# A long convolution's gates turned by VectorE through device memory, and its second inverse transform and norm done by rows

## The chip, the core and the metric

The kernel runs on one core of one Trainium2 chip. The core has five engines that run side by side and wait for each other by semaphores: TensorE (PE in the profile, with its weight loads as PEld) multiplies matrices, VectorE (DVE) and ScalarE (ACT) work elementwise, GpSimd (POOL) here mostly issues DMAs, and SyncE (SP) issues the other DMAs. Each engine takes its instructions in one fixed order; an instruction that waits holds everything behind it on the same engine. The metric is the device time of the whole program in microseconds (us). Times of the kernel before are the median of three runs.

## What is computed

One block of an encoder over 256 positions and 2048 features, in f32: a mix of four groups of 512 features each, then cross attention, then a gated feed-forward network, then a norm. The change touches the third group, a Hyena mixer:

```python
def hyena_mixer(u, conv_w, filt, skip):
    u = short_conv(u, conv_w).astype(jnp.float32)
    v, x1, x2 = jnp.split(u, 3, axis=-1)
    z = x1 * long_conv(v, filt[0], skip[0])
    return x2 * long_conv(z, filt[1], skip[1])
...
y_c = rms_norm(hyena_mixer(u_h, hy_conv_w[l], filt, hy_skip[l]), grp_norm_g[l, 1])
...
x = x + mix @ w_out[l]
```

`long_conv` is a convolution over all positions, done by a transform, a product and an inverse transform. `rms_norm` divides each position by the root mean square of its 512 features and multiplies by a gain for each feature.

## The kernel before

**Weights.** All large products go through one stream of weights. `Stream._half` (L73 to L106) loads slabs of 1 MB (`raw`, issued by SP at L81, three buffers) and splits each f32 weight in two halves of fewer bits: ScalarE rounds to `wh` (L102) and VectorE subtracts to get `wl` (L103). TensorE then multiplies three times (high by high, high by low, low by high) and sums in PSUM. One half slab is a tile of 128x1024; three buffers of `wh` and `wl` and a fourth that every fourth half uses let the splits run up to three halves ahead of TensorE. `gemm` (L296, L297) gives results with features on the partitions and positions along the row; `gemm_rows` (`part_rows`, L345 to L347) gives positions on the partitions and features along the row.

**Order of the rest.** The small work of the mixers is written as generators that hand over control with `yield`. `Background.poll` is called between the weight products and runs a step of a generator when enough TensorE time has passed since its last one and when VectorE is not thought to be behind (`owed`, which grows with each VectorE instruction announced by `dve` and falls with the TensorE time announced by `pe`). `drain` runs a generator to its end at once. The program's builder then orders each engine's instructions and sets the semaphores, so that small work lands between the weight products on TensorE and between the splits on ScalarE and VectorE.

**Hyena before.** `gemm("w_in", ...)` computes 12 tiles of 128 features by 256 positions: v (tiles 0 to 3), x1 (4 to 7), x2 (8 to 11). Each goes to `Hyena.feed` (L1057), which applies the short convolution (`conv3`, L599). For tiles 0 to 7 it then turns the tile with two TensorE transposes (L1067), one for even and one for odd times, so that time is on the partitions: v is split into two halves for the transforms, x1 is copied by ScalarE (L1076) to the tile `x1`. x2 stays with features on the partitions. The generator `convs` (L1238) makes the first transform (`spectrum`, `dft`, `triple` at L1106), the first inverse transform (12 products of 128x512, L1247 to L1261), the product with `x1`, the second transform, and then the second inverse transform: 16 products in full f32 whose results have 128 columns (L1280), with features on the partitions again, times x2, into `res[0]`. `group_norm` (L606) sums the squares over partitions with products by ones (L244), takes the inverse root with some twelve tiny VectorE instructions (`rstd_cols`), spreads it over the partitions with two products of 256 columns (L280), scales by it and by the gain, and splits the result into `act[16:20]` (L206 on ScalarE, L198 on VectorE).

**After Hyena.** Three `gemm_rows` follow the tile products: the values and the queries and keys of the GLA group, and the input of the FNet group. The queries and keys are turned by VectorE within blocks of 32x32 (`store_turned`, L380), stored to device memory by POOL (L382) and fetched back in the order wanted (`Gla.fetch`, L1330, 16 loads by POOL). This way of turning by a VectorE transpose, a store and a load with short runs is used for many other tiles (L382 and L387). Then all generators are drained, the buffers of Hyena are given up, and `Gla.open` takes their place with new tiles: it loads `gkw` (L1315) and `masks` (L1316) on SP and clears two tiles by POOL (L1318 to L1320). `gkw` is the right side of the products at L1337 that open the GLA group. `Fnet.open` loads its tables on SP (L1488). Last, `out_proj` multiplies `act[16:20]` (Hyena) first, then the GLA and FNet groups, then the last group.

Of the kernel before, what the change touches and what calls it, by code (L numbers as in the profile page):

```python
# [13 lines left out]
F32 = mybir.dt.float32  # L14
# [3 lines left out]
AF = mybir.ActivationFunctionType  # L18
ALU = mybir.AluOpType
# [3 lines left out]
P = 128  # L23
R = 256
# [18 lines left out]
LAG, OWED, SOON, FAR = 1.3, 0.9, 0.01, 18.0  # L43
V_NG = 0
V_GRP = 64
V_GLA = 76
V_GKB = 77
V_HCW = 81
V_SCW = 117
# [120 lines left out]
class Block:  # L170
# [219 lines left out]
    def run(self):  # L390
        nc, cp = self.nc, self.cp
        st = self.st
        self.act = [cp.tile([P, 512], F32R, name=f"act{i}") for i in range(24)]
        self.res = [cp.tile([P, 4, R], F32, name=f"res{i}") for i in range(4)]
        self.resk = lambda i: self.res[i // 4][:, i % 4, :]
        self.vec = cp.tile([P, NV], F32, name="vec")
        self.onesr = cp.tile([P, P], F32R, name="ones")
        self.ones = self.onesr.bitcast(F32)
        self.ident = cp.tile([P, P], F32, name="ident")

        self.sq = [cp.tile([P, 8], F32, name=f"sq{i}") for i in range(2)]
        self.mg = cp.tile([P, 16], F32, name="mg")
        self.eps = cp.tile([P, 8], F32, name="eps")[:, 0:1]
        self.gap(cp, 416)

        self.kd = self.outside("keys", KT)
        self.xf = [self.outside(n, KT) for n in ("features1", "features2")]
        self.qf = self.outside("queries", KT)
        self.sf, self.gf, self.gq = (self.outside(n, 4) for n in ("products", "gates", "gla"))
        self.ff = self.outside("hidden", FT)  # L410
        self.vd = nc.dram_tensor("values", (P, 8 * 512), F32, kind="Internal").ap()
        def load(src, k, n):
            nc.sync.dma_start(self.res[k // 4][:, k % 4:k % 4 + n, :].rearrange("p k r -> p (k r)"),
                              self.t[src][:, k * R:(k + n) * R])

        self.load_x = lambda k, n: load("xT", k, n)

        nc.vector.memset(self.ones, 1.0)

        p = self.bank()  # L420
        for _ in range(10):
            nc.tensor.matmul(p[:, 0:P], self.ones, self.ones, start=True, stop=True)
        nc.vector.memset(self.eps, EPS)
# [13 lines left out]
    def mixers(self):  # L437
        tc, nc, act = self.tc, self.nc, self.act
# [85 lines left out]
        with tc.tile_pool(name="mid", bufs=1) as mid:  # L524
# [41 lines left out]
            with tc.tile_pool(name="glp", bufs=1) as glp:  # L566
                gl.open(glp)
                fn.open(glp)
                g_fn = self.bg.add(fn.mix(act[0:4], gl))
                g_gla = self.bg.add(gl.mix(act[4:8]))  # L570
                halves = [(r, j) for r in range(2) for j in range(0, 512, R)]
                ps = self.gemm_rows("w_in", [US + 512], h)[0]
                c = [self.tmp() for _ in halves]
                for t, (r, j) in zip(c, halves):
                    nc.scalar.copy(t, ps[r][:, j:j + R])
                ps = self.gemm_rows("w_in", [US + 1024], h)[0]
                for t, (r, j) in zip(c, halves):
# [12 lines left out]
                def ev_s(i, p):  # L590
                    u0.append(i)
                    self.merge(p, self.res[1][:, i, :])

                self.gemm("w_in", [US + i * P for i in range(4)], h, ev_s)
                gl.done = True
                return self.out_proj(lambda n: self.bg.drain((g_fn, g_gla, g_sc)[n]))

    def conv3(self, u, c, y=None):
        y = self.tmp() if y is None else y  # L599
# [426 lines left out]
class Hyena:  # L1026
# [5 lines left out]
    def __init__(self, b, pool, k2):  # L1032
        self.b, self.k2, self.ready, self.pending = b, k2, False, None
        tile_ = lambda n, s, dt=F32: pool.tile(s, dt, name=n)
        self.tab = tile_("tab", [P, 512])
        self.tabh, self.tabl = (tile_(n, [P, 512], F32R) for n in ("tabh", "tabl"))

        self.backh, self.backl = (tile_(n, [P, 2 * P], F32R) for n in ("backh", "backl"))
        self.sp = [[[tile_(f"sp{o}{c}{k}", [P, 512]) for k in range(2)] for c in range(2)] for o in range(2)]
        self.x1 = tile_("x1", [P, 2, 512])  # L1040
        self.x2 = [tile_(f"x2{i}", [P, R]) for i in range(4)]

    def piece(self):
        return self.k2.tile([P, 512], F32, name="k2", tag="k2")
# [15 lines left out]
    def feed(self, i, u):  # L1060

        b, nc = self.b, self.b.nc
        if self.pending is not None:
            j, y = self.pending
            p = b.bank()
            for t in range(2):
                nc.tensor.transpose(p[:, t * P:(t + 1) * P], y[:, t, :], b.ident)  # L1067
            pv = p[:, 0:R].rearrange("p (t c) -> p t c", t=2)
            s = slice((j % 4) * P, (j % 4 + 1) * P)
            if j == 0:  # L1070
                self.z = [self.pair() for _ in range(2)]
            if j < 4:
                for par in range(2):
                    b.split2(*(d[:, s] for d in self.z[par]), pv[:, par, :])
            else:
                nc.scalar.copy(self.x1[:, :, s], pv)  # L1076
            self.pending = None
        if i < 8:
            self.pending = i, b.conv3(u, V_HCW + 3 * i).rearrange("p (i two) -> p two i", two=2)
# [165 lines left out]
    def convs(self):  # L1245
        b, nc = self.b, self.b.nc
        while not self.ready:  # L1247
            yield
        yield from self.spectrum(0)
        while self.fed < 9:  # L1250
            yield
        ps = []
        for par in range(2):
            y = [self.halves(self.y[cs][par]) for cs in range(2)]
            yield
            ps.append(b.bank())
            for cs in range(2):
                o = (2 * cs + 1) * P if par else cs * P
                th, tl = (self.tabh, self.tabl) if par else (self.backh, self.backl)
                self.triple(ps[par], th[:, o:o + P], tl[:, o:o + P], *y[cs], cs == 0, cs == 1)  # L1260
            b.bg.pe(1.4)  # L1261
# [10 lines left out]
        out = b.res[0]  # L1272
        nat = lambda x: x.rearrange("p (i two) -> p two i", two=2)
        sq = []
        for j in range(4):
            p = b.bank()
            s = slice(j * P, (j + 1) * P)
            for par in range(2):
                for cs in range(2):
                    nc.tensor.matmul(p[:, par * P:(par + 1) * P], self.y[cs][par][:, s], self.table(cs, par),  # L1280
                                     start=cs == 0, stop=cs == 1)
            b.tt(nat(out[:, j, :]), p[:, 0:R].rearrange("p (two i) -> p two i", two=2), nat(self.x2[j]), ALU.mult)
            if j % 2:
                yield
        yield from b.group_norm(out, 1, b.act[16:20])


class Gla:
# [358 lines left out]
```

## Time and profile before

| | us |
|---|---|
| median of three runs | 1471.92 (1471.43 to 1472.27) |
| the profiled execution, its own time | 1471.97 |
| its span, from the first to the last instruction of the core | 1470.2 |
| TensorE busy in that span | 1460.1 |
| VectorE busy | 929.6 |
| ScalarE busy | 746.3 |
| GpSimd busy | 179.3 |

The profile page gives busy times, a strip of the span in 40 slices, the chain of waits that ended last, and the costliest groups. The trace behind it can be asked for windows (busy time of each engine in a stretch), for a timeline of one engine, for the instructions of one source line, for waits and for DMAs. In a timeline a line shows the start, the time of the merged instructions, the engine, the source line, the operation, `out<-in` by tile names, sizes, the count and, in brackets, the idle time before and what ended it. Matmuls overlap in their pipeline, so the distance from one start to the next, not the duration shown, is what a matmul costs.

### The profile page before, as it was taken

The page shows a single profiled execution, that of the slowest core. Times are in us where ns is not written, and L with a number is a line of the kernel's source. Part 1 is how long each engine was busy: PE and PEld are TensorE (multiplying, and loading weights), DVE is VectorE, ACT ScalarE, POOL GpSimd, SP SyncE. Part 2 cuts the span into 40 slices and gives each one's busy share as a digit, 9 for nine tenths or more (in the row PEclk, how much of TensorE's full clock was granted, in tenths as well). Part 3 has the DMA queues.
Part 4 walks back from the last instruction along what each step waited for, and adds up shares of the span by engine and source line. Part 5 has one row for each costly group of instructions (what it writes and reads, how often), then busy time and mean ns, then how long its engine had stood idle before and what let it go on. Part 6 is the DMA issues. An engine that isn't in the chain of part 4 may idle for free.

```text
span 1470.2 us, 18237 instructions
## 1 busy us (share of the span) xinstructions
PE 1460.1 (99%) x6832; PEld 1216.9 (83%) x6832; DVE 929.6 (63%) x1344; ACT 746.3 (51%) x1079; POOL 179.3 (12%) x240
## 2 busy tenths in 40 slices
PE   9999999999999999999999999999999999999997
PEld 7888888888888888888888888888888888888886
DVE  6777768777778685886765554555555456444445
ACT  6566655446656464665554444444444445434344
POOL 0000000022121223410501100111110011000000
PEclk9999999999999999999999999999999999999999
DMA  9877554455556778764856666666666666555554
GB/s 351 300 280 252 201 194 164 156 203 195 201 180 216 237 244 250 242 184 149 269 181 225 225 206 203 224 229 218 216 220 210 215 211 227 198 185 193 197 200 144
DMA packets 58329, 315.98 MB, mean 215 GB/s; under 512 B 8925, under 2 KB 10622, under 8 KB 26624
## 3 DMA queue, kind: packets, MB, share of 16 engines
q1 hardware_dynamic: 46064, 281.11, 55.5%
q0 software_dynamic: 11744, 33.04, 8.5%
q8 instruction: 53, 0.87, 0.2%
q10 hardware_dynamic: 432, 0.66, 0.1%
q14 instruction: 36, 0.29, 0.1%
HBM read 296.43 MB, written 18.35 MB: 214 GB/s over the span
## 4 chain that ended last, share of the span: by engine, by line
PE 96%; ACT 1%; DVE 1%; DMA 1%; issue 0%; SPq 0%; ACTq 0%
PE pg L345 26%; PE pg L346 26%; PE pg L347 26%; PE pg L296 7%; PE pg L297 4%; PE pm L347 1%; PE pm L345 1%; PE pm L346 1%; PE pm L1106 1%; PE pm L874 1%; PE pm L846 1%; DMA raw<-in_W 0%; DVE wl L103 0%; DMA tmp<-in_cfn 0%; ACT wh L102 0%
## 5 line engine op out<-in xcount | busy, mean ns | idle before, releaser
L103 DVE TENSOR_TENSOR wl<-raw,wh 128x1024 fp32r<-128x1024 f32 (+1 forms) x503 | 611.4, 1216 | 471.1 <-ACT wh L102 470.2
L102 ACT CAST wh<-raw 128x1024 fp32r<-128x1024 f32 (+1 forms) x503 | 523.9, 1043 | 585.6 <-PE pg L347 503.5
L345 PE MATMUL pg<-wh,act 128*128 128x512 f32 (+1 forms) x1562 | 610.8, 391 | 0.6 <-ACT wh L102 0.6
L346 PE MATMUL pg<-wl,act 128*128 128x512 f32 (+1 forms) x1562 | 608.8, 390 | 0.6 <-DVE wl L103 0.5
L347 PE MATMUL pg<-wh,act 128*128 128x512 f32 (+1 forms) x1562 | 608.8, 390 | 0.0
L345 PEld LDWEIGHTS pg<-wh,act 128*128 128x128 f32 x1562 | 293.3, 188 | 63.0 <-issue 1.2
L346 PEld LDWEIGHTS pg<-wl,act 128*128 128x128 f32 x1562 | 293.5, 188 | 61.7 <-DVE wl L103 2.1
L347 PEld LDWEIGHTS pg<-wh,act 128*128 128x128 f32 x1562 | 293.3, 188 | 61.3
L296 PE MATMUL pg<-act,wh 128*128 128x512 f32 x432 | 152.0, 394 | 0.0
L297 PE MATMUL pg<-act,wl 128*128 128x256 f32 x432 | 121.2, 281 | 0.0
L296 PEld LDWEIGHTS pg<-act,wh 128*128 128x128 f32 x432 | 81.2, 188 | 17.4
L297 PEld LDWEIGHTS pg<-act,wl 128*128 128x128 f32 x432 | 81.3, 188 | 0.2
L382 POOL DMA_DIRECT2D hidden<-u x22 | 16.7, 762 | 408.0 <-DVE u L380 408.0
L345 PE MATMUL pg<-wh,f 128*128 128x512 f32 x120 | 46.7, 390 | 0.0
L347 PE MATMUL pg<-wh,f 128*128 128x512 f32 x120 | 46.7, 389 | 0.0
L346 PE MATMUL pg<-wl,f 128*128 128x512 f32 x120 | 46.7, 389 | 0.0
L387 POOL DMA_DIRECT2D tmp<-hidden x44 | 38.8, 888 | 41.3 <-ACT wh L102 16.9
L382 POOL DMA_DIRECT2D features<-tmp x24 | 17.0, 715 | 82.9 <-DVE tmp L380 82.9
L347 PEld LDWEIGHTS pg<-wh,f 128*128 128x128 f32 x120 | 22.5, 188 | 4.7
L346 PEld LDWEIGHTS pg<-wl,f 128*128 128x128 f32 x120 | 22.5, 188 | 4.7
L345 PEld LDWEIGHTS pg<-wh,f 128*128 128x128 f32 x120 | 22.5, 188 | 4.6
L901 ACT ACTIVATE g<-pg,rc 128x512 f32<-128x512 f32 x22 | 15.0, 689 | 9.6 <-PE pg L347 9.6
(313 smaller groups left out, 1132.8 us busy)
## 6 DMA issues: line engine op xcount, KB each, us to landing
raw<-in_W SPq DMA_DIRECT2D x246, 1024.0 KB, 4.9
raw<-in_W SPq DMA_DIRECT2D x11, 512.0 KB, 7.1
hidden<-u POOLq DMA_DIRECT2D x22, 256.0 KB, 3.5
tmp<-hidden POOLq DMA_DIRECT2D x44, 128.0 KB, 4.5
features<-tmp POOLq DMA_DIRECT2D x24, 128.0 KB, 2.5
res<-in_xT SPq DMA_DIRECT2D x5, 512.0 KB, 6.2
ar<-features POOLq DMA_DIRECT2D x20, 128.0 KB, 6.0
k<-in_mem SPq DMA_DIRECT2D x8, 256.0 KB, 8.3
```

The costliest lines, as they stand in the source:

```text
L102: nc.scalar.copy(wh[:, a:b], r[:, a:b])
L103: nc.vector.tensor_tensor(out=wl[:, a:b], in0=r[:, a:b], in1=wh[:, a:b].bitcast(F32), op=ALU.subtract)
L296: self.nc.tensor.matmul(p[:, :], wh, slot[:, :], start=start, stop=False)
L297: self.nc.tensor.matmul(p[:, 0:R], wl, slot[:, 0:R], start=False, stop=stop)
L345: self.nc.tensor.matmul(p, hi, wh, start=start, stop=False)
L346: self.nc.tensor.matmul(p, hi, wl, start=False, stop=False)
L347: self.nc.tensor.matmul(p, lo, wh, start=False, stop=stop)
L382: self.nc.gpsimd.dma_start(to[r], u.rearrange("p (k c) -> p k c", c=P))
L387: self.nc.gpsimd.dma_start(t.rearrange("p (g t) -> p g t", t=32), src)
L846: nc.tensor.matmul(p[:, :], q[d][:, r * P:(r + 1) * P], kt[d][:, :], start=d == 0, stop=False)
L874: nc.tensor.matmul(p[:, :], vh[m][:, s], pt[m][:, :], start=m == 0, stop=False)
L901: nc.scalar.activation(g[r], ps[r], AF.Silu, scale=box["col"][:, r:r + 1])
```

## The change

x1 and x2 (tiles 4 to 11) are no longer turned by TensorE or left as they are. After the short convolution, `turn` transposes the even times and the odd times of the tile with two VectorE instructions of 128x128 (within blocks of 32x32) and sends the result through device memory: one store and two loads by POOL, so that time is on the partitions, even times apart from odd times. The second inverse transform is now the same as the first (`back`, 12 products of 128x512 with split operands) and leaves time on the partitions and features along the row. Its result is multiplied by x2 (VectorE), squared and summed along the row (ScalarE), scaled (ScalarE), turned by VectorE, stored to device memory and loaded back to `res[0]` with features on the partitions; the gain and the split into `act[16:20]` follow in a new generator `long_conv` among the work of the next groups. The gains and the rows of `w_out` are put into the matching order on the host.

```diff
@@ run
+        self.hf = self.outside("long", 4)
+        self.hy = [nc.dram_tensor(f"times{i}", (R, P), F32, kind="Internal").ap() for i in range(8)]
@@ mixers
                 fn.open(glp)
+                self.bg.add(self.long_conv())
                 g_fn = self.bg.add(fn.mix(act[0:4], gl))
...
+    def long_conv(self):
+        nat = lambda x: x.rearrange("p (i two) -> p two i", two=2)
+        yield 14
+        for k in range(4):
+            x = self.res[0][:, k, :].rearrange("p (two i) -> p two i", two=2)
+            hi, lo = (nat(self.act[16 + k][:, c:c + R]) for c in (0, R))
+            g = self.gvec(V_GRP + 4, k)
+            mark = self.mark()
+            self.nc.scalar.activation(hi, x, AF.Copy, scale=g)
+            self.stt(lo, x, g, hi.bitcast(F32), ALU.mult, ALU.subtract)
+            self.keep_place(mark)
+            yield SOON
@@ Hyena.__init__
-        self.x1 = tile_("x1", [P, 2, 512])
-        self.x2 = [tile_(f"x2{i}", [P, R]) for i in range(4)]
+        self.x1, self.x2 = (tile_(n, [P, 2, 512]) for n in ("x1", "x2"))
@@ Hyena.feed
-            if j < 4:
-                for par in range(2):
-                    b.split2(*(d[:, s] for d in self.z[par]), pv[:, par, :])
-            else:
-                nc.scalar.copy(self.x1[:, :, s], pv)
+            for par in range(2):
+                b.split2(*(d[:, s] for d in self.z[par]), pv[:, par, :])
             self.pending = None
-        if i < 8:
-            self.pending = i, b.conv3(u, V_HCW + 3 * i).rearrange("p (i two) -> p two i", two=2)
+        y = b.conv3(u, V_HCW + 3 * i)
+        if i < 4:
+            self.pending = i, y.rearrange("p (i two) -> p two i", two=2)
         else:
-            b.conv3(u, V_HCW + 3 * i, self.x2[i - 8])
+            self.turn(y, b.hy[i - 4], (self.x1, self.x2)[i // 8], i % 4)
         self.fed = i + 1
+
+    def turn(self, y, d, to, j):
+        b, nc = self.b, self.b.nc
+        u = b.tmp()
+        b.bg.dve(R, 2)
+        for par, x in enumerate(y.rearrange("p (f b two) -> p two b f", b=4, two=2)[:, i] for i in range(2)):
+            nc.vector.transpose(u[:, par * P:(par + 1) * P].rearrange("p (b f) -> p b f", b=4), x)
+        nc.gpsimd.dma_start(d.rearrange("(t p) c -> p t c", p=P), u.rearrange("p (t c) -> p t c", c=P))
+        for par in range(2):
+            nc.gpsimd.dma_start(to[:, par, j * P:(j + 1) * P].rearrange("p (g t) -> p g t", t=32),
+                                d[par * P:(par + 1) * P].rearrange("(g f) (b t) -> (f b) g t", f=32, t=32))
@@ Hyena.convs, after the second transform
-        for j in range(4):
-            p = b.bank()
-            s = slice(j * P, (j + 1) * P)
-            for par in range(2):
-                for cs in range(2):
-                    nc.tensor.matmul(p[:, par * P:(par + 1) * P], self.y[cs][par][:, s], self.table(cs, par),
-                                     start=cs == 0, stop=cs == 1)
-            b.tt(nat(out[:, j, :]), p[:, 0:R].rearrange("p (two i) -> p two i", two=2), nat(self.x2[j]), ALU.mult)
-            if j % 2:
-                yield
-        yield from b.group_norm(out, 1, b.act[16:20])
+        ps = []
+        yield from self.back(ps)
+        rows = b.res[0].rearrange("p k r -> p (k r)")
+        col = b.rp.tile([P, 8], F32, name="sm", tag="sm")[:, 0:2]
+        rows = [rows[:, par * 512:(par + 1) * 512] for par in range(2)]
+        for par, x in enumerate(rows):
+            b.tt(x, ps[par], self.x2[:, par, :], ALU.mult)
+            nc.scalar.activation(ps[par], x, AF.Square, accum_out=col[:, par:par + 1])
+            yield SOON
+        yield
+        y = b.rstd_cols(col, 512)
+        for par, x in enumerate(rows):
+            nc.scalar.activation(x, x, AF.Copy, scale=y[:, par:par + 1])
+            yield
+            b.store_turned(b.hf, 0, par, self.piece(), x)
+        for k in range(4):
+            b.load_turned(b.res[0][:, k, :], b.hf, k)
+
+    def back(self, ps):
+        b = self.b
         for par in range(2):
             y = [self.halves(self.y[cs][par]) for cs in range(2)]
             yield
             ps.append(b.bank())
             for cs in range(2):
                 o = (2 * cs + 1) * P if par else cs * P
                 th, tl = (self.tabh, self.tabl) if par else (self.backh, self.backl)
                 self.triple(ps[par], th[:, o:o + P], tl[:, o:o + P], *y[cs], cs == 0, cs == 1)
             b.bg.pe(1.4)
@@ kernel (host side)
-    for a, n in ((V_GRP + 8, 4), (V_GLA, 1), (V_SCW, 12)):
+    for a, n in ((V_GRP + 4, 8), (V_GLA, 1), (V_SCW, 12)):
...
-    for a in (0, 1536):
+    for a in (0, 1024, 1536):
         src["w_out"][a:a + 512] = turned(src["w_out"][a:a + 512])
```

More of the change, by code (lines that the diff above doesn't have):

```diff
@@ L1271, in convs @@
             yield
-        out = b.res[0]
-        nat = lambda x: x.rearrange("p (i two) -> p two i", two=2)
-        sq = []
-        for j in range(4):
-            p = b.bank()
-            s = slice(j * P, (j + 1) * P)
-            for par in range(2):
-                for cs in range(2):
-                    nc.tensor.matmul(p[:, par * P:(par + 1) * P], self.y[cs][par][:, s], self.table(cs, par),
-                                     start=cs == 0, stop=cs == 1)
-            b.tt(nat(out[:, j, :]), p[:, 0:R].rearrange("p (two i) -> p two i", two=2), nat(self.x2[j]), ALU.mult)
-            if j % 2:
-                yield
-        yield from b.group_norm(out, 1, b.act[16:20])
+        ps = []
+        yield from self.back(ps)
+        rows = b.res[0].rearrange("p k r -> p (k r)")
[15 more added lines that the diff above has]
+        b = self.b
+        for par in range(2):
+            y = [self.halves(self.y[cs][par]) for cs in range(2)]
+            yield
+            ps.append(b.bank())
+            for cs in range(2):
+                o = (2 * cs + 1) * P if par else cs * P
+                th, tl = (self.tabh, self.tabl) if par else (self.backh, self.backl)
+                self.triple(ps[par], th[:, o:o + P], tl[:, o:o + P], *y[cs], cs == 0, cs == 1)
+            b.bg.pe(1.4)
 class Gla:
```

6 lines of the change are left out of this document (removed).

## The prediction

> **What bounds it.** I read the page first, then TensorE's waits, then its timeline where the change cuts in.
>
> ```profile
> span 1470.2 us, 18237 instructions
> PE 1460.1 (99%) x6832; PEld 1216.9 (83%) x6832; DVE 929.6 (63%) x1344; ACT 746.3 (51%) x1079; POOL 179.3 (12%) x240
> PE 96%; ACT 1%; DVE 1%; DMA 1%; issue 0%; SPq 0%; ACTq 0%
> PE pm L422 <- DVE eps L423: 1.1, 1, 1.1
> PE pg L345 <- ACT wh L102: 0.6, 1, 0.6
> PE pg L346 <- DVE wl L103: 0.5, 2, 0.3
> ```
>
> The first two lines are the span and the busy times, the third the chain that ended last, the others all the waits of TensorE that the trace lists, as a total, a count and the longest. TensorE is busy 99% of the span, the chain is TensorE for 96%, and its listed waits come to 2.2 us. None belongs to Hyena, so nothing can be gained there by removing a wait. What this change is worth is the TensorE time that it takes away or adds, plus whatever new waits it makes.
>
> The price of a product is the distance between starts:
>
> ```profile
> 270.90 0.39 PE L1106 MATMUL pm<-w3h,backh 128*128 128x512 f32 x1
> ...
> 272.28 0.39 PE L345 MATMUL pg<-wh,act 128*128 128x512 f32 x1
> ```
>
> Six products of 512 columns (one `triple` for both `cs`) from 270.90 to 272.28: 1.38 us, 0.23 each. A product of 256 columns is taken at half of it, 0.115.
>
> **Removed from TensorE.** Eight transposes (a pair for each of x1's four tiles), sixteen products of 128 columns in two groups, then the sums and the spread of `group_norm`:
>
> ```profile
> 230.20 0.39 PE L1067 MATMUL pm<-ident,tmp 128*128 128x128 f32 x2
> 230.35 0.47 PE L296 MATMUL pg<-act,wh 128*128 128x512 f32 x1
> 230.66 0.28 PE L297 MATMUL pg<-act,wl 128*128 128x256 f32 x1
> ...
> 247.69 0.40 PE L296 MATMUL pg<-act,wh 128*128 128x512 f32 x1
> 247.98 0.48 PE L1067 MATMUL pm<-ident,tmp 128*128 128x128 f32 x2
> ...
> 248.41 0.40 PE L296 MATMUL pg<-act,wh 128*128 128x512 f32 x1
> ...
> 310.56 1.95 PE L1280 MATMUL pm<-tab,k 128*128 128x128 f32 x16
> 312.26 0.48 PE L345 MATMUL pg<-wh,act 128*128 128x512 f32 x1
> 312.58 0.39 PE L346 MATMUL pg<-wl,act 128*128 128x512 f32 x1
> ...
> 325.76 0.50 PE L244 MATMUL pm<-ones,tmp 128*128 128x1 f32 x4
> ...
> 326.89 0.39 PE L345 MATMUL pg<-wh,act 128*128 128x512 f32 x1
> ...
> 334.38 0.28 PE L280 MATMUL pm<-dgh,ones 128*128 128x256 f32 x1
> ...
> 335.31 0.40 PE L345 MATMUL pg<-wh,act 128*128 128x512 f32 x1
> ```
>
> The first weight product behind such a block starts late too (312.26 to 312.58 is 0.32, not 0.23), so I measure to the second one and subtract the weight products in between.
> - Transposes: the first pair 230.20 to 230.66 is 0.46, less 0.23, is 0.23. Around the last, 247.69 to 248.41 holds one product of 512 columns ahead and one of 256 behind: 0.72 less 0.345 is 0.375. Mean 0.30, four pairs 1.21. Bounds: twice the 0.11 a piece of the products of the same size (1.79/16, next item), four times 0.22 = 0.9; or the 0.48 shown as the duration of a pair, 1.9.
> - Second inverse: 310.56 to 312.58 is 2.02, less 0.23, is 1.79; two such groups 3.58.
> - Sums L244: 325.76 to 326.89 is 1.13 with three weight products in it (0.69): 0.44. Spread L280: 334.38 to 335.31, 0.93 less 0.69: 0.24.
>
> Sum removed 5.47. **Added:** twelve products of 512 columns, two times the 1.38 above: 2.76. Net -2.71 us: the span of 1470.2 loses that, the 1.77 around it stays, and the profiled execution's 1471.97 becomes 1469.26. The median of before lies 0.05 under that execution, so against the median 1469.2.
>
> In sentences that the sum can do without: the Trainium skill, TensorE: Matmul & The Clock Gate, Part 4: PE-mode transpose, gives about 275 ns for a 128x128 transpose in one kernel's context. By that, eight are 2.2 us and the sum would be 1468.2. The rows above show a pair for 0.23 to 0.375, so the sum goes by them. The Trainium skill, VectorE: DVE Perf Modes, Rules for kernel authors, speaks against the edit itself: for a 128x128 transpose it says to use TensorE if a PSUM destination is OK. What that would cost here hangs on VectorE's room, which comes next.
>
> **VectorE.** It gets two transposes for each of eight tiles, in about 226 to 268 us, among the splits that feed TensorE.
>
> ```profile
> 232.00:246.00 14.00, 14.00 (x83) 12.25 (x83) 13.93 (x22) 8.12 (x14) 0.00 (x0) 1.00 0.50 159
> 246.00:268.00 22.00, 22.00 (x147) 18.25 (x146) 19.47 (x29) 11.39 (x18) 0.00 (x0) 1.00 0.53 187
> 268.00:290.00 22.00, 22.00 (x100) 18.03 (x97) 14.05 (x18) 10.18 (x14) 0.00 (x0) 1.00 0.44 144
> L380 DVE STREAM_TRANSPOSE tmp<-res x24: 398/402/440, 498.2 to 723.1; 128x256 f32<-128x256 f32 x24
> L380 DVE STREAM_TRANSPOSE u<-h x22: 664/684/701, 787.8 to 1223.6; 128x512 f32<-128x512 f32 x22
> ```
>
> The windows give length, then busy time of PE, PEld, DVE, ACT and POOL, granted clock, DMA share and GB/s. The L380 rows give 402 ns for 256 columns and 684 for 512: 1.10 ns a column and 0.12 us fixed, so 128 columns cost an estimated 0.26 (lower end 0.20, half of 402; upper end 0.40, if the stride of two makes 128 cost as much as 256). Sixteen are 4.2 us, 3.2 to 6.4. I take 4.2, since `store_turned` also reads in pieces. VectorE has 0.07 + 2.53 = 2.6 us free from 232 to 268, so 1.6 us doesn't fit, and 268 to 290 has 7.95 free. What becomes late is not the split first: each turn is announced (`bg.dve`), and `poll` holds back Hyena's own steps, the two spectra. In the order of the changed program the first inverse transform stands some 34 TensorE instructions later, and the transpose comes between the splits, which may run up to three half slabs ahead. So I cost it at nothing; the cover is that lead. Without it, it is the 4.2 us (rival D).
>
> The rest of VectorE and ScalarE changes kind rather than size: on VectorE two products and two transposes of 512 columns and four splits come in where four products, three sums and four splits went; ScalarE loses the four copies of x1 and four squares and gets two squares, two scales and the four `act[16:20]` halves later. Between the two halves of the second `back` stand twelve weight products (2.8 us); in them come two casts and two subtractions, about 0.69 each. One split of 1.23 in their way makes 3.2 and a wait of 0.4. The first inverse transform has the same shape and shows no wait. I take 0.2, from 0 to 0.4.
>
> **GpSimd and its DMAs.** Each turn is one store and two loads on a queue that was empty until 312 (POOL 0.00 in all three windows).
>
> ```profile
> features<-tmp POOLq DMA_DIRECT2D x24, 128.0 KB, 2.5
> hidden<-u POOLq DMA_DIRECT2D x22, 256.0 KB, 3.5
> keys<-k POOLq DMA_DIRECT2D x8, 256.0 KB, 7.3
> gg<-in_gkw SPq DMA_DIRECT2D x1, 256.0 KB, 2.6
> tmp<-in_cfn SPq DMA_DIRECT2D x3, 128.0 KB, 4.9
> 320.17 2.85 POOL L382 DMA_DIRECT2D gla<-tmp  x4
> ...
> 333.79 4.73 POOL L1330 DMA_DIRECT2D res<-gla  x7 [0.27 <-DMA res<-gla]
> ```
>
> The last column of the first five is the median from issue to landing. An issue costs 0.71 (2.85/4) or 0.68 (4.73/7). A tile needs 0.71 for its store, 2.5 to 3.5 until that has landed (POOL waits, the loads behind it), and 1.36 for two loads: 4.6 to 5.6 us. Tiles come every (247.98-230.20)/3 = 5.9 us, so POOL keeps up. x1 is wanted at 271 and x2 at about 325; the last tiles of each come over ten us before. Cost 0; if every store took 7.3, a tile would need 9.4 us, x1 would be there at about 228 + 4 x 9.4 = 266 and x2 at 303, still in time.
>
> **The new wait.** `gkw` takes the place of Hyena's buffers, which now end with the two stores to `long`. So the SP load of `gkw` has to wait for both, and behind it on SP stands the next slab; the four products at L1337 wait for it, and all of TensorE's weight products behind them.
>
> ```profile
> 344.95 0.33 SPq L81 DMA_DIRECT2D raw<-in_W  x1
> 350.31 1.03 PE L1337 MATMUL pm<-lr,gg 128*128 128x256 f32 x4
> 326.30 0.16 DVE L255 TENSOR_SCALAR rc<-pm 128x2 f32<-128x2 f32 x1 [1.39 <-PE pm L244]
> ...
> 329.46 0.16 DVE L202 SCALAR_TENSOR_TENSOR rc<-rc 128x2 f32<-128x2 f32 x1
> 329.58 1.23 DVE L103 TENSOR_TENSOR wl<-raw,wh 128x1024 fp32r<-128x1024 f32 x1
> L198 DVE TENSOR_TENSOR k<-k,k 128x512 f32<-128x512 f32 x8 | 5.5, 686 | 0.0
> L978 ACT ACTIVATE res<-res,rc 128x512 f32<-128x512 f32 x4 | 2.7, 716 | 1.3 <-DVE rc L972 1.3
> ```
>
> In the changed order L1337 stands three weight products earlier, so at about 350.31 - 0.69 - 2.71 = 346.9, and 81 weight products, 18.6 us, after the end of the second inverse transform (328.3). In these 18.6 us must go: product with x2 0.69, square 0.72 (as a scale of that size), root 3.3 (326.30 to 329.62), two scales 1.43, transpose 0.68, store 3.5, load 2.6: 12.9, and up to three splits of 1.23 in between: 16.6. POOL's sixteen loads for GLA, which come ahead of the stores, end at 338.5 on the old clock; from there a second store and the load end at 338.5 + 0.7 + 3.5 + 2.6 = 345.3. Both are in time, by 1.7 to 2 us. On SP, `gkw` now stands just ahead of the slab issued at 344.95, and the stores have landed by 342.7 in this count, so the slab isn't held. I cost this at 0, bounded from above by a store of 7.3 (+3.8) and a load of 4.9 (+2.3): 22.7, late by 4.1 us. A store of 7.3 alone is late by 1.8. No row of before has this chain, and SP and POOL are both shared, so it is the weakest place of the sum.
>
> In a sentence by itself: the Trainium skill, DMA: Bandwidth & Descriptors, Anatomy of one DMA, fits 2.0 us plus the bytes over 436 KB a us, an estimate of 2.6 for 256 KB, with which store and load would end 0.9 earlier than with the 3.5 above. The rows of before, 2.6, 3.5 and 7.3 for the same 256 KB, don't let me lean on it.
>
> **Rivals.**
> - B, the `gkw` load is late by 1 to 4 us and TensorE stands at L1337: 1469.4 + 1 to 4, so 1470.4 to 1473.4, with the 1.8 of a slow store 1471.2. For it: the slack is only 2 us and the spread of stores (3.5 to 7.3) is larger. Against it: the chain as counted already carries three splits.
> - C, the removed blocks cost TensorE more than the distances show: a pair of transposes at its duration of 0.48 (1.9 instead of 1.21), and no wait at `back`: 1469.2 - 0.7 = 1468.5. For it: 0.375 at the last pair shows that a pair's cost varies, and two of four aren't in the rows. Against it: matmuls overlap, so a duration overstates.
> - D, slower: VectorE has no room from 232 to 268, where it is busy 13.93 of 14 us, and each transpose delays the next split. It decides once the lead of three halves is used up. None absorbed: 1469.2 + 4.2 = 1473.4; at 0.40 a transpose 1475.6. For it: the window. Against it: 7.95 us free right behind, no wait on `wl` there before though 13.93 was used, and the held-back spectra.
> - E, nothing comes of it, since what TensorE saves is waited for at a split or a slab later: 1471.9. Against it: TensorE waits 1.1 us for splits in the whole span, so the splits are ahead nearly always, and what is removed here is busy time, not cover for a wait.
>
> **The numbers.** Forecast A, the sum with 0.2 at `back`: 1469.4, own range 1468.9 to 1470.3. Chances: A 0.45, C 0.22, B 0.20, D 0.10, E 0.03. The range leaves out D and the edges of B and C: 1468.3 to 1472.8. What a measurement tells from no change is about 0.2%, 2.9 us: faster is under 1469.0, slower over 1474.9. Faster: C and 0.05 of A, 0.27. Slower: the upper half of D, 0.05, and B if D's start adds to it, 0.06, together 0.11. Same: 0.62.
>
> **What would show it.** Right: the page's busy time of TensorE about 2.7 lower; no row of waits at the products with gg (now near 347); VectorE near full from 226 to 268 and fuller than before from 268 to 290; first inverse transform later by some us without a wait. B would show as a wait of TensorE for a DMA into gg, 1 to 4 us long, with SP's issue of `gkw` after 343. D would show as waits for wl at L297 or L346 between 230 and 290. C would show as less TensorE busy than the sum. The forecast is wrong if a wait of over 1 us stands anywhere but at the start, or if the new `back` costs more than 1.38 for its six products.

## The result: 1479.25 us, slower by 0.4%

| | us |
|---|---|
| before, median of five runs beside it | 1472.27 |
| changed kernel, median of five runs (1477.01 to 1480.13) | 1479.25 |
| ratio, 95% interval (the medians divide to 1.0047) | 1.004 (1.0029 to 1.0051) |
| changed kernel, profiled execution: own time and span | 1477.49 and 1475.7 |

The profiled execution is 1.8 us under the median of its kernel, so the traces explain 5.5 us of span (1475.7 against 1470.2); the rest of the 7 us between the medians has no trace.

The page of the changed kernel, its first lines, then all waits of TensorE that the trace lists (total, times, longest):

```profile
span 1475.7 us, 18244 instructions
PE 1460.2 (99%) x6798; PEld 1214.2 (82%) x6798; DVE 933.6 (63%) x1355; ACT 746.9 (51%) x1078; POOL 202.3 (14%) x270
...
PE pg L346 <- DVE wl L103: 5.8, 6, 1.6
PE pm L424 <- DVE eps L425: 1.1, 1, 1.1
PE pm L1371 <- DMA gmask<-in_masks: 0.3, 1, 0.3
```

TensorE has 34 instructions fewer, yet the same busy time, though the removed products were worth 2.7 us. Part of what a wait costs is counted as busy, since the next starts are slower too (1.5 us, by the waits below). Waits for wl went from 0.5 to 5.8 us. To see where, I compare the start of the same weight product in both traces. First the 902nd, the 1472nd and the last weight product of before, then of the changed kernel:

```profile
215.67 0.28 PE L297 MATMUL pg<-act,wl 128*128 128x256 f32 x1
...
347.81 0.39 PE L346 MATMUL pg<-wl,act 128*128 128x512 f32 x1
...
1462.00 0.39 PE L347 MATMUL pm<-held,act 128*128 128x512 f32 x1
```

```profile
215.80 0.28 PE L297 MATMUL pg<-act,wl 128*128 128x256 f32 x1
...
345.14 0.39 PE L346 MATMUL pg<-wl,act 128*128 128x512 f32 x1
...
1467.05 0.39 PE L347 MATMUL pm<-held,act 128*128 128x512 f32 x1
```

Ahead of the change the new kernel is 0.13 us behind. At 345 it is 2.67 ahead, so the stretch with all the removed and added products brought 2.80 us. After that it loses 7.7. The products of L1371, where `gkw` is used, and the waits behind them, in TensorE's timeline (in brackets the idle time and what ended it):

```profile
346.73 0.39 PE L347 MATMUL pg<-wh,act 128*128 128x512 f32 x1
347.47 1.10 PE L1371 MATMUL pm<-lr,gg 128*128 128x256 f32 x4 [0.35 <-DMA gmask<-in_masks]
...
359.14 0.50 PE L346 MATMUL pg<-wl,act 128*128 128x512 f32 x1 [0.55 <-DVE wl L103]
363.76 0.50 PE L346 MATMUL pg<-wl,act 128*128 128x512 f32 x1 [1.59 <-DVE wl L103]
368.61 0.50 PE L346 MATMUL pg<-wl,act 128*128 128x512 f32 x1 [1.09 <-DVE wl L103]
373.16 0.50 PE L346 MATMUL pg<-wl,act 128*128 128x512 f32 x1 [1.49 <-DVE wl L103]
380.31 0.50 PE L346 MATMUL pg<-wl,act 128*128 128x512 f32 x1 [0.65 <-DVE wl L103]
```

These six waits are 5.7 us, and some 7.2 by the distances of the starts around them, against 0.23 for a product that doesn't wait. All stand at the place where `gkw` is used or behind it. Why the splits are late there, SP's timeline shows first, then ScalarE's:

```profile
344.06 0.33 SPq L1349 DMA_DIRECT2D gg<-in_gkw  x1
344.44 0.43 SPq L1350 DMA_DIRECT2D gmask<-in_masks  x1
344.96 0.37 SPq L81 DMA_DIRECT2D raw<-in_W  x1
345.39 1.37 SPq L1522 DMA_DIRECT2D tmp<-in_cfn  x3
```

```profile
348.17 0.47 ACT L1374 ACTIVATE gw<-pm,vec 128x256 f32<-128x256 f32 x1 [1.96 <-PE pm L1371]
355.40 0.81 ACT L214 CAST fth<-tmp 128x256 fp32r<-128x256 f32 x2 [6.75 <-DMA tmp<-in_cfn]
356.12 0.47 ACT L1374 ACTIVATE gw<-pm,vec 128x256 f32<-128x256 f32 x1
356.48 0.39 ACT L214 CAST fch<-tmp 128x256 fp32r<-128x256 f32 x1
356.78 1.05 ACT L102 CAST wh<-raw 128x1024 fp32r<-128x1024 f32 x1
```

Before, the same two places read:

```profile
345.33 1.68 SPq L1488 DMA_DIRECT2D tmp<-in_cfn  x3
...
350.37 0.40 ACT L214 CAST fth<-tmp 128x256 fp32r<-128x256 f32 x1 [1.48 <-DMA tmp<-in_cfn]
```

The loads of `cfn` go out at 345.39, as before (345.33), but now right behind `gkw`, the masks and a slab, and beside four loads from `long` on POOL. The DMA view, last column issue to landing, gives before:

```profile
tmp<-in_cfn SPq DMA_DIRECT2D x3, 128.0 KB, 4.9
```

and for the changed kernel:

```profile
res<-long POOLq DMA_DIRECT2D x4, 128.0 KB, 8.1
tmp<-in_cfn SPq DMA_DIRECT2D x3, 128.0 KB, 9.9
```

The five us that `cfn` is later are the five that ScalarE stands longer at its cast (6.75 against 1.5 before), and the next rounding of a slab (L102 at 356.78) stands behind that cast. That uses up the lead of the splits, and they stay late until 381. That is the theory to test; the rival is that VectorE and ScalarE simply have more to do from 355 to 390, where the four pieces of `long_conv` came among the steps of GLA.

### The profile page after: what moved, and what is told of

Read it like the earlier page. It is cut to its first block, busy times and chain, and to the rows that moved or that the text cites. A ratio compares the mean times of both kernels' runs of the same rounds, so it can differ in the third digit from the quotient of the medians.

```text
span 1475.7 us, 18244 instructions
## 1 busy us (share of the span) xinstructions
PE 1460.2 (99%) x6798; PEld 1214.2 (82%) x6798; DVE 933.6 (63%) x1355; ACT 746.9 (51%) x1078; POOL 202.3 (14%) x270
## 4 chain that ended last, share of the span: by engine, by line
PE 96%; ACT 1%; DMA 1%; DVE 1%; issue 0%; SPq 0%; ACTq 0%
PE pg L345 25%; PE pg L346 25%; PE pg L347 25%; PE pg L296 7%; PE pg L297 4%; PE pm L345 1%; PE pm L346 1%; PE pm L347 1%; PE pm L1132 1%; DMA tmp<-in_cfn 1%; PE pm L891 1%; PE pm L863 0%; DMA raw<-in_W 0%; DVE wl L103 0%; ACT wh L102 0%
## 5 line engine op out<-in xcount | busy, mean ns | idle before, releaser
L102 ACT CAST wh<-raw 128x1024 fp32r<-128x1024 f32 (+1 forms) x503 | 523.7, 1042 | 580.2 <-PE pg L347 502.2
L546 POOL DMA_DIRECT2D values<-tmp x16 | 8.6, 542 | 88.6 <-ACT tmp L545 88.6
```

The costliest lines, as they stand in the source:

```text
L102: nc.scalar.copy(wh[:, a:b], r[:, a:b])
L546: nc.gpsimd.dma_start(self.vd[:, o:o + R], v)
```

## The experiments

Medians of the kernel and of the kernel before beside it, with the ratio and its 95% interval:

| run | us | before | ratio |
|---|---|---|---|
| e1_tmp: stores to `long` from `tmp` tiles | 1477.56 | 1472.22 | 1.0037 (1.0025 to 1.005) |
| e2_cfn: `cfn` loaded early | 1472.79 | 1472.22 | 1.0001 (0.9992 to 1.001) |
| e3_lateloads: loads of `long` later | 1478.43 | 1472.22 | 1.0042 (1.0029 to 1.0054) |
| e4_x1only: kernel before, x1 alone by VectorE | 1471.3 | 1472.22 | 0.9994 (0.9985 to 1.0002) |
| e5_both: `tmp` tiles, and the call for `cfn` moved | 1477.27 | 1472.36 | 1.0038 (1.0025 to 1.005) |
| e6_lateuse: casts of `cfn` later | 1474.75 | 1472.36 | 1.0016 (1.0007 to 1.0025) |
| e7_x2only: x2 alone by VectorE | 1473.77 | 1472.36 | 1.0012 (1.0002 to 1.0021) |
| e8_noloads: no loads of `long` | 1475.65 | 1472.36 | 1.0025 (1.0015 to 1.0036) |
| e9_res: turned halves in `res[1]` | 1471.65 | 1472.28 | 0.9995 (0.9986 to 1.0004) |
| e10_rescfn: `res[1]` and `cfn` early | 1469.8 | 1472.28 | 0.998 (0.9971 to 0.9989) |
| e11_double: the last one, transposes doubled | 1469.47 | 1472.28 | 0.998 (0.9972 to 0.9989) |

### cfn earlier, gkw as it is

```diff
                 fn = Fnet(self, act[20:24])
+                fn.load()
...
+    def load(self):
+        b = self.b
+        self.x = [b.tmp() for _ in range(3)]
+        for i, x in enumerate(self.x):
+            b.nc.sync.dma_start(x, b.t["cfn"][:, i * R:(i + 1) * R])
...
```

> Only the place of the three `cfn` loads changes: they are issued before the product of the FNet group, three slabs ahead of `gkw`, which still waits for the stores to `long`. Theory: ScalarE no longer stands at `cfn`, so the waits for wl between 350 and 390 go (under 1 us), while a wait for `gkw` or the masks at the first product of GLA stays, 0.3 to 1.5 us: 1471 to 1474. Rival (more work on VectorE and ScalarE from 355 to 390): waits for wl stay at 4 us or more, 1476 to 1480.

The tables are issued at 313 in place of 345. No wait for wl is left between 350 and 390, the wait for `gkw` and the masks is larger (they are issued from 345.96 on here):

```profile
PE pm L1372 <- DMA gmask<-in_masks: 1.7, 1, 1.7
PE pg L346 <- DVE wl L103: 1.6, 4, 0.8
```

Of the 1.6, 0.76 stands at 589 and the rest in the first 14 us. The time fell by 6.5 us, to that of before, as expected; only the wait for the masks is a little above its 1.5. The added work of VectorE and ScalarE is all there in this run, so that rival falls.

### The casts of cfn later, all loads as they are

```diff
+        self.x = []
...
-            o = i % 2 * R
-            b.split2(d[0][:, o:o + R], d[1][:, o:o + R], x)
+            self.x.append((d, i % 2 * R, x))
...
-        yield 10
+        yield 9
+        mark = b.mark()
+        for d, o, x in self.x:
+            b.split2(d[0][:, o:o + R], d[1][:, o:o + R], x)
+        b.keep_place(mark)
+        yield 2
```

> The changed kernel with all loads at their places; only ScalarE's three casts of `cfn` (and VectorE's three subtractions) stand three roundings of slabs later. Theory (ScalarE stands at `cfn` and holds the roundings behind it): `cfn` still lands 8 to 10 us after issue, but ScalarE doesn't wait for it, and the waits for wl between 350 and 375 fall from 4.7 to under 1.5 us: 1471 to 1475. Rival (the slab issued between the masks and `cfn` lands late itself, so the roundings would have waited for it in any case): ScalarE waits for raw instead, wl waits stay at 4 us or more, 1477 to 1480.

`cfn` still took 9.9 us to land. In ScalarE's timeline a rounding now comes at 351.82, where the changed kernel's came at 356.78, so the slab had been there and the cast alone held it back:

```profile
351.82 1.03 ACT L102 CAST wh<-raw 128x1024 fp32r<-128x1024 f32 x1
...
357.39 1.98 ACT L102 CAST wh<-raw 128x1024 fp32r<-128x1024 f32 x2
359.27 0.71 ACT L214 CAST fth<-tmp 128x256 fp32r<-128x256 f32 x2
```

Waits of TensorE for wl are 0.2 us in the whole span, the wait for the masks is 2.2. The median fell by 4.5 us, to the upper part of the expected range. The loads and their landing are those of the changed kernel; only the order of the instructions differs, so what held the splits there was the place of the casts on ScalarE. The order changed on TensorE too: the first products of GLA now stand nine weight products earlier (behind 1470 of them, not 1479), about 2 us, which is why they wait longer for the masks. The profiled execution is the fastest of its eleven, 2.1 us under the median: from the 902nd to the last weight product it takes 0.3 us less than before, where the changed kernel takes 4.9 more, and what its median costs beyond that has no trace.

### gkw without the wait for the stores

First by storing from `tmp` tiles, then the same with `fn.load()` of the early `cfn` added, here behind the FNet group's product and not ahead of it:

```diff
-            b.store_turned(b.hf, 0, par, self.piece(), x)
+            for j in range(0, 512, R):
+                b.store_turned(b.hf, j // P, par, b.tmp(), x[:, j:j + R])
```

> The two stores to `long` read from `tmp` tiles (four pieces of 256 columns) and no longer from a tile of the memory that `gkw` takes, so the load of `gkw` has only the product with x2 to wait for. Theory: the late `gkw` load pushes the masks, a slab, the `cfn` tables and the four loads of `long` into the same few us; `cfn` lands 10 us after its issue, ScalarE stands at the cast of `cfn` for 6.8 us with the next rounding of a slab behind it, and TensorE waits 6 us for wl and 0.5 for the masks. Then with this edit: `gkw` issued before 340, no wait for masks, ScalarE's wait for `cfn` under 2 us, TensorE's waits for wl between 350 and 390 under 1 us, time 1470 to 1472. Rival (VectorE and ScalarE have more to do from 355 to 390, with the four pieces of `long_conv` among the work of GLA): waits for wl there stay at 4 us or more, time 1476 to 1480.

> Both edits together: the stores to `long` from `tmp` tiles, so that `gkw` is loaded early, and the three `cfn` loads three slabs earlier. Theory (two late loads are all that the change costs): no wait for `gkw` or the masks, no waits of TensorE for wl between 350 and 390, ScalarE waits for `cfn` under 0.5 us. In this order, as in the run with the first edit alone, the last spread of a norm (L280) stands right ahead of the product that needs it, which cost 3.0 us there: 1469.5 to 1473.5, by whether that wait is there. Rival (the added work of VectorE and ScalarE): waits for wl at 4 us or more, 1475 or more.

Both medians missed the expectation. `gkw` was issued at 330.9 and 330.0, no wait for the masks was left, and around 350 to 390 the waits for wl were gone. The second run doesn't do what its expectation says: with the call behind the product, `cfn` went out at 342.57, hardly earlier than the 343.15 of the first run, and ScalarE waited for it 3.4 us (2.7 in the first), not under 0.5. So it is close to a repeat of the first. But the finer pieces made the builder order TensorE's products anew, and the last spread of a norm (L280) came to stand right ahead of the product that needs it. In the run with `tmp` pieces alone:

```profile
485.77 0.28 PE L280 MATMUL pm<-dgl,ones 128*128 128x256 f32 x1
489.05 0.50 PE L345 MATMUL pg<-wh,act 128*128 128x512 f32 x1 [2.99 <-ACT act L206]
```

By the starts of the same weight products this place cost 3.5 us in the first of the two runs and 5.1 in the second. The idle time is 2.99 us in both. Behind it the granted clock of TensorE stayed at 1.00 in the first trace; in the second it read 0.50 from 489 to 492, with the starts 0.43 us apart in place of 0.23, which is the rest. So the medians could not price the late `gkw`; they show what an edit that only moves instructions can cost here.

The next pair writes the two turned halves to `res[1]`, idle at that time, which leaves TensorE's order around GLA as in the changed kernel:

```diff
-            b.store_turned(b.hf, 0, par, self.piece(), x)
+            b.store_turned(b.hf, 0, par, b.res[1].rearrange("p k r -> p (k r)")[:, par * 512:(par + 1) * 512], x)
```

> The two transposes whose result goes to `long` write to `res[1]`, which is idle then, and no longer to the memory that `gkw` takes. TensorE's order of products stays that of the changed kernel (the four products with gg and the last spread of a norm at the same places), which the run with `tmp` pieces didn't keep. Theory (the late load of `gkw` and what it drags along is all the harm): `gkw` issued before 335, no wait for the masks, `cfn` landing 6 to 7 us after issue, waits for wl between 350 and 390 under 1.5 us: 1470.5 to 1473.5. Rival (the added work among GLA's steps): waits for wl at 4 us or more, 1476 or more.

> The same and the three `cfn` loads three slabs earlier. Theory: no wait for either load, waits for wl under 1 us; the sum of removed and added products, -2.7 us, is then nearly all there, less up to 1 us of small waits in the cross attention: 1469.5 to 1471.5, faster than before. Rival: something else in the changed kernel costs as much as the products gain, 1472 to 1474.

With the early `gkw` alone (issued at 331.41) the time is 1471.65, inside the expectation, though two of its signs missed: `cfn`, still at its old place, took 8.0 us to land and not 6 to 7, ScalarE stood 2.7 us, and two waits for wl of 1.51 and 0.67 were left, 2.2 in place of under 1.5. With `cfn` early too it is 1469.8, inside the expectation and faster than before with the whole interval. Its waits of TensorE, all but the first within 8 to 15 us, and the three products used above:

```profile
PE pm L424 <- DVE eps L425: 1.1, 1, 1.1
PE pg L346 <- DVE wl L103: 0.9, 3, 0.5
PE pg L345 <- ACT wh L102: 0.4, 1, 0.4
...
217.13 0.28 PE L297 MATMUL pg<-act,wl 128*128 128x256 f32 x1
...
346.47 0.39 PE L346 MATMUL pg<-wl,act 128*128 128x512 f32 x1
...
1460.40 0.39 PE L347 MATMUL pm<-held,act 128*128 128x512 f32 x1
```

This execution was late by 1.46 us at the 902nd product, from its start; from there to the 1472nd it gains 2.80, as the changed kernel did, and to the end 3.06. Here nothing of it is given back.

### One half of the change at a time

x1 turned by VectorE in the kernel before, and x1 left to TensorE in the changed kernel:

```diff
-        if i < 8:
+        if i < 4:
             self.pending = i, b.conv3(u, V_HCW + 3 * i).rearrange("p (i two) -> p two i", two=2)
+        elif i < 8:
+            self.turn(b.conv3(u, V_HCW + 3 * i), b.hy[i - 4], self.x1, i % 4)
```

> The kernel before with x1 alone turned by VectorE and device memory; x2, the second inverse transform and the norm as before. By the sum: eight transposes less on TensorE, -1.2 us, nothing for VectorE's eight transposes: 1471.1 (1470.5 to 1471.8). Rival (VectorE is full from 232 to 268, so that each transpose delays a split): not faster than before, 1472.3 to 1474.4, with waits for wl at L297 between 230 and 290.

```diff
-        if i < 4:
+        if i < 8:
             self.pending = i, y.rearrange("p (i two) -> p two i", two=2)
...
-            for par in range(2):
-                b.split2(*(d[:, s] for d in self.z[par]), pv[:, par, :])
+            if j < 4:
+                for par in range(2):
+                    b.split2(*(d[:, s] for d in self.z[par]), pv[:, par, :])
+            else:
+                nc.scalar.copy(self.x1[:, :, s], pv)
```

> The changed kernel with x1 turned by TensorE as before and x2 alone by VectorE: the second half of the change by itself. Theory (all the harm lies in the second half; x1's part gains 0.9 to 1.2): 1479.5 to 1481, with the waits for wl between 350 and 390 as in the changed kernel. Rival (the turns of x1 push the later work back and are part of the harm): under 1478.5.

x1 alone brought 0.9 us between the medians, inside the expected band, though the interval still touches no change; in its trace the stretch from the 902nd to the 1472nd weight product is 1.24 us shorter than before. The second half alone missed: 1473.77, not 1479.5 or more, so the rival holds, by which the turns of x1 are part of the harm. Its trace shows `gkw` issued at 341.17 (344.06 in the whole change), no wait for the masks, and `cfn` landing after 6.9 us; ScalarE stood 2.4 us:

```profile
341.17 0.33 SPq L1352 DMA_DIRECT2D gg<-in_gkw  x1
...
343.88 0.33 SPq L81 DMA_DIRECT2D raw<-in_W  x1
344.25 2.83 SPq L1525 DMA_DIRECT2D tmp<-in_cfn  x3
```

So the halves don't add: +1.4 and -0.9 apart, +7.0 together. The turns of x1 cost TensorE no wait where they stand. But with them the last store to `long` goes out at 338.62 (337.42 without them) and takes 5.2 us to land (3.6 without), so `gkw` is issued 2.9 us later, and the second half has no lead to lose.

### Which transfers delay cfn

```diff
-        for k in range(4):
-            b.load_turned(b.res[0][:, k, :], b.hf, k)
```

> The changed kernel without the four loads from `long`: the Hyena result is not brought back with features on the partitions, so that part of the output is left out. Theory (`gkw`, the masks and a slab ahead of `cfn` on SP are enough): `cfn` lands 8 to 10 us after its issue, 1477 to 1480. If the four loads with their short runs hold the DMA engines: landing 5 to 6.5 us, waits for wl under 2 us, 1471 to 1475.

`cfn` landed in 7.3 us, between the two answers expected, and the time, 1475.65, lies between them too. Without the four loads about half of the five us of extra landing is gone, so they are part of the cause. The shares are not told apart, though: with `res[1]`, where the four loads are there and `gkw` and the masks had gone out 12 us before, `cfn` took 8.0 us. With x1 alone, where there is no `long` and `gkw` had gone out 15 us before, it took 6.3, and 4.9 in the kernel before. An earlier run moved the four loads into `long_conv`:

> The four loads of `long` are issued later, from inside `long_conv`, so that they don't share the DMA engines with `cfn`; `gkw` waits as in the changed kernel. Theory: four requests less in front of or beside `cfn`, which still shares with `gkw`, the masks and a slab: `cfn` lands 6 to 8 us after issue instead of 10, half of the waits for wl go, 1473 to 1476. If the loads of `long` alone delay `cfn`: landing 5 us, 1471 to 1473. If they have nothing to do with it: landing 10 us, 1478 to 1480.

It tells nothing apart. The loads went out at 348.12, only 3.7 us later, still beside `cfn` (9.9 us). And the FNet group's result took `res[0]` (from 388.2) before the Hyena result there was split (from 392.6), so in this run the Hyena part of `act` holds other values.

### Does VectorE have room

This edit stands on top of the last kernel with `res[1]` and the early `cfn` (1469.8 us):

```diff
         for par, x in enumerate(y.rearrange("p (f b two) -> p two b f", b=4, two=2)[:, i] for i in range(2)):
-            nc.vector.transpose(u[:, par * P:(par + 1) * P].rearrange("p (b f) -> p b f", b=4), x)
+            for _ in range(2):
+                nc.vector.transpose(u[:, par * P:(par + 1) * P].rearrange("p (b f) -> p b f", b=4), x)
```

> As the last one, with each of the sixteen transposes of x1 and x2 done twice into the same place: 6.6 us more on VectorE between 227 and 275, unannounced to the pacing. If the lead of the splits covers VectorE's work there: no wait of TensorE between 226 and 290, within 0.7 us of the run before it. If VectorE is at its limit there: waits for wl at L297 or L346 between 240 and 290, 2 to 6 us slower than the run before it.

No wait of TensorE between 226 and 290, and 1469.47 against 1469.8. The windows of this run (length, then busy PE, PEld, DVE, ACT, POOL, clock, DMA share, GB/s):

```profile
226.00:246.00 20.00, 20.00 (x114) 17.34 (x113) 19.69 (x39) 10.13 (x15) 5.20 (x7) 1.00 0.52 186
246.00:268.00 22.00, 22.00 (x147) 18.29 (x145) 22.00 (x43) 10.25 (x16) 8.23 (x11) 1.00 0.65 215
268.00:290.00 22.00, 22.00 (x98) 18.12 (x97) 17.58 (x26) 10.62 (x14) 4.48 (x6) 1.00 0.59 194
```

VectorE is all but full for 42 us, with twice the transposes, and TensorE doesn't wait. Nor do Hyena's own products move: the first inverse transform starts 60.8 us behind the 902nd weight product in this run, in the one without the doubling, and in the changed kernel. The added work went into VectorE's free time; from 268 to 290 it is busy 17.58 us, where it was 13.89 without the doubling.

## Why the prediction was wrong

**The step that failed** is the sentence on SP in "The new wait": that `gkw` stands just ahead of the slab, that the stores have landed by then, and that this costs 0. The 342.7 for the stores is reckoned in the order of the changed kernel, but 344.95, against which it is held, is the time of the slab in the trace of before. TensorE is 2.7 us ahead there, so the slab is due 2.7 earlier. The best kernel, where nothing holds SP, issues it at

```profile
343.61 0.33 SPq L81 DMA_DIRECT2D raw<-in_W  x1
```

and runs 1.33 us behind the changed kernel from its start, so there the slab was due at 342.3; it went out at 344.96. By the count's own 342.7 the slab, and `cfn` behind it, were already held. The sentence asked whether `gkw` is late for its product and whether the slab behind it is held. It didn't go one further in the queue, to the three `cfn` loads, nor from there to ScalarE, whose cast of `cfn` stands ahead of the rounding of a slab. Rival B, with chance 0.20, had the right load, and its sign came true (SP issues `gkw` after 343), but a wrong price: its own wait is 0.35 us (0.5 by the starts), and the harm, five waits for wl of 5.4 us, is what came out of SP at once behind it. Delaying only the casts, or issuing only `cfn` early, takes back 4.5 and 6.5 us.

**The sum of products** was right. Forecast -2.71, measured -2.80 in the changed kernel and in the best one (the 0.2 for a wait at `back` did not come); for x1 alone the sum says -1.21 and the trace -1.24. So rival C, by which the removed blocks cost more, is not needed.

In a sentence by itself: the figure of 275 ns a transpose from the Trainium skill, TensorE: Matmul & The Clock Gate, Part 4: PE-mode transpose, would have made it -3.7, an estimate; these traces don't bear it out, since the eight gave 1.24 us, 0.155 each.

**VectorE** was mis-sized and still free. A 128x128 transpose took 0.41 us, not the 0.26 estimated nor within the end of 0.40:

```profile
L1104 DVE STREAM_TRANSPOSE tmp<-tmp 128x128 f32<-128x128 f32 x16 | 6.0, 412 | 0.0
```

(in a group's row: busy time, then mean ns). The sixteen keep VectorE busy for 6.0 us, not 4.2; their durations overlap a little and add up to 6.6. No wait of TensorE came of it, and doubling them changed nothing, so rival D falls. The first product of the first inverse transform did go from 270.90 to 276.59, but by the order of the program (it stands behind 1206 weight products in place of 1176) and not by VectorE's time, since doubling the transposes doesn't move it. The forecast had counted that order: it put the end of the second inverse transform at 328.3, and it came at 328.6.

**The chain to gkw.** Predicted: stores landed by 342.7 and `gkw` there at 345.3. In the trace the second store was issued at 338.62, near the 338.5 counted, but that is luck: 338.5 was to be the end of POOL's loads for GLA, which ended at 333.95, and the store waited for VectorE's transpose. That one ended at 338.32, where the other count, the chain with three splits, gives 338.8. What was off in the sum is the store, here by the DMA view of the second one alone:

```profile
long<-k POOLq DMA_DIRECT2D x1, 256.0 KB, 5.2
```

I took 0.7 and 3.5 from the row of `hidden<-u`, 4.2 in all, though my upper end had 7.3. So SP could issue `gkw` only at 344.06, 5.4 us after the store, and the masks behind it ended TensorE's wait. Rival E, that nothing is gained since other waits take it up, was given 0.03 with the argument that the splits are ahead nearly always. They were, until one other load on ScalarE's order took the lead away.

Open: about 0.8 us that the changed kernel loses in the cross attention, between 590 and 620, in many short gaps, and the 1.8 us between its profiled run and its median. In the other traces that stretch costs from 0 (x1 alone, the second half alone) to 2.3 us (`cfn` earlier) against before, so it need not belong to the change. Open too is which transfers make `cfn` land late, and by how much each.

## What to carry to other kernels

When a load has to wait longer than before, price not its own use but everything issued behind it on the same queue, and for each of those ask which engine stands at its first use and what critical work is queued there. When two times are compared, take both from the same order: a time read from the trace of before moves by what the change saves ahead of it. A step that costs nothing where it stands can still delay what depends on it: follow it to the first thing that has no lead. The cast of a constant table cost nothing here when its load was issued three slabs early; with the load landing late, ScalarE stood 6.75 us ahead of it, with the roundings that feed TensorE behind.

## What the runs showed that was not expected

The same load landed twice as late among others: `cfn` took 4.9 us behind a slab alone, 9.9 behind `gkw`, the masks and a slab with four loads by POOL beside them, and 7.3 without those four. This is no rule by count, as the 8.0 and 6.3 us of the other runs show. The Trainium skill, DMA: Bandwidth & Descriptors, Issuing engines are not separate DMA queues, says that DMAs issued by different engines run on the same 16 DMA engines and interleave. The step from 9.9 to 7.3, when POOL's loads are left out, agrees with it.

The start of a run is not steady: the 902nd weight product, ahead of every edit, began at 215.67 to 217.13 in the four traces of before, of the whole change, of x1 alone and of the best kernel, with the waits for the first splits. That is larger than the gain of x1 alone, so differences between traces were taken from one product to a later one, not from the span.
